# The bias tables of an attention mixer move out of the first feed-forward to the memory's keys, and 1/rms begins behind the second chunk

## The chip, the cores and the metric

The kernel runs on one core of one Trainium2 chip. The metric is the device time of one execution in microseconds (us), as the median of several runs of the same program.

## The reference

Two transformer layers over 512 positions of width 1024, with float32 tensors. What matters here:

```python
# layer 1
x = x + 0.5 * swiglu_ffn(rmsnorm(x, g1), w_in1, w_out1)        # f1, width 2816
h = rmsnorm(x, g_mix)
o_nsa  = nsa_attention(..., rel_bias)   # scores + rel_bias[rel_bucket(distance)]
o_conv = short_gated_conv(...)
o_mem  = memory_attention(...)          # keys and values from 256 memory rows
x = x + (g_nsa * o_nsa + g_conv * o_conv + g_mem * o_mem) @ w_out
x = x + 0.5 * swiglu_ffn(rmsnorm(x, g2), w_in2, w_out2)        # f2
# layer 2: sliding window and linear attention, memory attention, then
x = x + swiglu(rmsnorm(x, g3), w_gate, w_up, w_down)           # f3
return rmsnorm(x, g_final)
```

`rel_bias` has 32 buckets for 16 heads. A distance decides the bucket, so the bias of a head is one line of numbers over the distances, and the attention needs that line in each of 128 partitions.

## The kernel before

**Matmuls.** Each product is made of three, of the high and the low half of both sides (`mm3`, L233). A weight of 512 KB is fetched by SyncE's queue (SP) into one of three raw buffers, `wr`; ScalarE (ACT) casts its high half, `wh` (L260); the low half `wl` is a subtraction (L242) on VectorE (DVE), or, in the two mixers, on GpSimd (POOL) for two weights of three and on DVE for the third. TensorE (PE) then runs the matmuls, all recorded in line 231; `chunk` (L313) is one output tile of 24 matmuls. A scheduler lays out the order on each engine when the program is built; `tick` (L541) lets the next step of a list, `self.todo`, be written at that point, and `issue_after` holds a step until after a given matmul.

**Feed-forwards.** f1, f2 and f3 have one form (`ffn`, L688): three plain chunks (`plain`, L656), then 19 chunks as `unit` with fewer multiplications, whose weights `f_s` are summed by a second DMA on POOL's queue, and after each of three groups of chunks eight output products, which end in the DVE instruction `x<-u,x` (L254). The norm's 1/rms is made while the first chunks run: `rc` (L443) sums squares by eight small matmuls `o<-ones,acc`, and makes the root by some twelve small DVE instructions (`rsv`, `rs4t`, `rs4y`) and the cast `rsh` on ACT; `rb` (L449) spreads the result by matmuls with `identr`.

**Tables.** `tables` (L511) makes 16 steps, one after each of f1's chunks or output products. Eight are `line` steps for a quarter of a table: each opens a pool `tab`, sets and loads `rel` (POOL's queue, L520), loads a piece of the one-hot matrix `oh` (SP, L522), makes one product into the PSUM buffer `o`, copies it to `row` on DVE, and writes that to DRAM (`drel` or `dcmp`, POOL's queue, L527). Eight are `rows` steps: POOL's queue writes two heads' lines for 128 partitions, 640 KB, from `drel` to `dline` in DRAM (L533).

**Memory attention in the first mixer.** `mix1` (L1420) calls `mem_kv` (L867): eight chunks of keys (weights `m_km`), each scaled to `kr` and squared to `ksq`; eight pieces of weights for the values (`m_vm`); then the keys' own root of mean squares (`mem_rms`, matmuls `t<-im,ksq`, twelve DVE instructions, two transposes, `hr`) and eight matmuls `t<-hr,bm` that scale the keys. `mem_heads` (L958) then does scores, softmax and sums of four heads, with gate products from weights `m_gm` beside them.

## Time and profile before

| | us |
|---|---|
| median of three runs (2512.44, 2512.69, 2516.0) | 2512.69 |
| the profiled execution | 2515.75 |
| its span in the trace | 2514.0 |
| PE busy | 2373.9 |
| DVE, ACT, POOL busy | 1698.5, 1159.3, 442.9 |

The span is what the trace shows from the first instruction to the last, and 1.75 us of the profiled execution lie around it. In a row, the engine, the line and the operation are followed by the output tile and its inputs; an entry in square brackets is idle time before the instruction, with what ended it. PEclk is the granted clock of TensorE, 1.00 at 2.4 GHz and 0.50 at 1.2 GHz.

### The profile page before, as it was taken

The page shows a single profiled execution, that of the slowest core. Times are in us where ns is not written, and L with a number is a line of the kernel's source. Part 1 is how long each engine was busy: PE and PEld are TensorE (multiplying, and loading weights), DVE is VectorE, ACT ScalarE, POOL GpSimd, SP SyncE. Part 2 cuts the span into 40 slices and gives each one's busy share as a digit, 9 for nine tenths or more (in the row PEclk, how much of TensorE's full clock was granted, in tenths as well). Part 3 has the DMA queues.
Part 4 walks back from the last instruction along what each step waited for, and adds up shares of the span by engine and source line. Part 5 has one row for each costly group of instructions (what it writes and reads, how often), then busy time and mean ns, then how long its engine had stood idle before and what let it go on. Part 6 is the DMA issues. An engine that isn't in the chain of part 4 may idle for free.

```text
span 2514.0 us, 35498 instructions
## 1 busy us (share of the span) xinstructions
PE 2373.9 (94%) x13626; PEld 2054.5 (82%) x13626; DVE 1698.5 (68%) x3149; ACT 1159.3 (46%) x2072; POOL 442.9 (18%) x279
## 2 busy tenths in 40 slices
PE   8974999899999999999999999998999998999997
PEld 6864998797778887887899998787788887789997
DVE  6733778766487757777676776467877367866675
ACT  5412445344355444444553453454665345643453
POOL 1101000242122223222000001212121431000000
PEclk8986999999999999999999999999999999999999
DMA  6525554343122222223445554222222332545551
GB/s 180 171 82 134 160 148 148 98 146 99 56 80 70 75 64 73 74 68 126 126 148 142 157 142 128 74 66 70 67 68 75 115 122 76 136 145 147 157 140 61
DMA packets 100165, 277.45 MB, mean 110 GB/s; under 512 B 18403, under 2 KB 26923, under 8 KB 99868
## 3 DMA queue, kind: packets, MB, share of 16 engines
q1 hardware_dynamic: 82924, 239.81, 29.3%
q0 software_dynamic: 17072, 35.38, 7.4%
q8 instruction: 107, 1.75, 0.3%
q14 instruction: 62, 0.51, 0.1%
HBM read 268.69 MB, written 11.64 MB: 112 GB/s over the span
## 4 chain that ended last, share of the span: by engine, by line
PE 64%; DVE 10%; ACT 3%; issue 2%; DMA 1%; POOL 0%; DVEq 0%; ACTq 0%; POOLq 0%
PE g L231 36%; PE s L231 12%; PE t L231 11%; PE o L231 3%; PE t L239 2%; DVE wl L242 2%; ACT wh L260 1%; DMA wr<-f_s 1%; DVE qk L242 0%; DVE sp L1269 0%; DMA wr<-f_o 0%; DVE cv L254 0%; DVE sm L242 0%; ACT qk L260 0%; DVE o L254 0%
## 5 line engine op out<-in xcount | busy, mean ns | idle before, releaser
L231 PE MATMUL g<-xs,wh 128*128 128x512 f32 (+1 forms) x3022 | 886.4, 375 | 6.9 <-ACT wh L260 4.0
L260 ACT CAST wh<-wr 128x1024 fp32r<-128x1024 f32 (+6 forms) x405 | 409.7, 1015 | 625.3 <-PE g L231 209.1
L231 PEld LDWEIGHTS g<-xs,wh 128*128 128x128 f32 x3022 | 546.7, 191 | 97.7 <-ACT wh L260 7.2
L231 PE MATMUL g<-xs,wl 128*128 128x512 f32 (+1 forms) x1511 | 564.2, 373 | 1.4 <-POOL wl L242 1.2
L242 POOL TENSOR_TENSOR wl<-wr,wh 128x1024 fp32r<-128x1024 f32 (+4 forms) x135 | 313.8, 2325 | 901.3 <-ACT wh L260 671.6
L242 DVE TENSOR_TENSOR wl<-wr,wh 128x1024 fp32r<-128x1024 f32 (+5 forms) x270 | 326.8, 1211 | 81.8 <-ACT wh L260 79.6
L231 PEld LDWEIGHTS g<-xs,wl 128*128 128x128 f32 x1511 | 288.8, 191 | 52.2 <-issue 2.9
L231 PE MATMUL s<-xs,wh 128*128 128x256 f32 (+1 forms) x890 | 225.5, 341 | 8.0 <-ACT xs L260 2.0
L231 PE MATMUL t<-xs,wh 128*128 128x512 f32 (+1 forms) x888 | 224.1, 341 | 0.5 <-ACT e L260 0.4
L561 POOL DMA_DIRECT2D wr<-f_s x57 | 49.4, 872 | 775.8 <-DVE wl L242 174.1
L231 PEld LDWEIGHTS s<-xs,wh 128*128 128x128 f32 x890 | 154.2, 191 | 31.2 <-ACT wh L260 4.2
L231 PEld LDWEIGHTS t<-xs,wh 128*128 128x128 f32 x888 | 153.5, 190 | 20.1 <-ACT e L260 1.2
L231 PE MATMUL t<-xs,wl 128*128 128x512 f32 (+1 forms) x444 | 151.6, 341 | 2.7 <-DVE wl L242 2.7
L231 PE MATMUL s<-xs,wl 128*128 128x256 f32 (+1 forms) x445 | 151.2, 340 | 0.0
L257 ACT ACTIVATE sp<-sp,nm 128x128 f32<-128x128 f32 x192 | 101.9, 532 | 54.3 <-DVE nm L1269 41.5
L242 DVE TENSOR_TENSOR ptl<-t,pth 128x512 fp32r<-128x512 f32 (+1 forms) x128 | 73.4, 603 | 55.5 <-ACT pth L260 55.2
L260 ACT CAST pth<-t 128x512 fp32r<-128x512 f32 (+1 forms) x128 | 62.1, 520 | 92.7 <-PE t L239 92.3
L231 PE MATMUL g<-th,wh 128*128 128x256 f32 x308 | 86.6, 281 | 9.3 <-ACT wh L260 8.8
L231 PEld LDWEIGHTS t<-xs,wl 128*128 128x128 f32 x444 | 84.4, 190 | 13.2 <-DVE wl L242 4.0
L231 PEld LDWEIGHTS s<-xs,wl 128*128 128x128 f32 x445 | 85.0, 191 | 8.8
L231 PE MATMUL g<-th,wl 128*128 128x256 f32 x308 | 86.9, 282 | 1.6 <-DVE wl L242 1.5
L231 PE MATMUL g<-tl,wh 128*128 128x256 f32 x308 | 86.0, 279 | 0.0
(524 smaller groups left out, 4820.3 us busy)
## 6 DMA issues: line engine op xcount, KB each, us to landing
wr<-f_ab SPq DMA_DIRECT2D x73, 512.0 KB, 3.7
wr<-f_s SPq DMA_DIRECT2D x57, 512.0 KB, 3.6
wr<-f_s POOLq DMA_DIRECT2D x57, 512.0 KB, 7.0
wr<-f_o SPq DMA_DIRECT2D x48, 448.0 KB, 3.4
wr<-m_f SPq DMA_DIRECT2D x40, 512.0 KB, 3.6
wr<-m_o SPq DMA_DIRECT2D x40, 512.0 KB, 3.6
w<-f_ab SPq DMA_DIRECT2D x57, 256.0 KB, 4.2
wr<-f_o SPq DMA_DIRECT2D x24, 512.0 KB, 5.1
```

The source lines that it names most:

```text
L231: self.pm = self.nc.tensor.matmul(o, l, r, start=first, stop=last, skip_group_check=more)
L239: self.nc.tensor.transpose(o, i, self.ident)
L242: (e or self.nc.vector).tensor_tensor(o, x, y, op=op)
L257: return self.nc.scalar.activation(o, x, f, **k)
L260: return self.nc.scalar.copy(o, x)
L561: nc.gpsimd.dma_start(rs, a[key + "_s"][c][:, D:], accum_op=ALU.add)
```

## The change

**Tables.** `run` no longer puts the steps into f1. `mix1` opens one pool `tab` on the right around `mem_kv`, and eleven steps are written from there, one after each chunk of keys, and what is left behind the values. `rel` is loaded once, the two one-hot matrices come whole by SP, four matmuls (two of 320 columns, two of 512) go to the PSUM buffer `t`, four DVE copies make the tables, POOL's queue writes `drel` and `dcmp` once each, and the eight broadcasts `dline` follow.

**1/rms.** In all three feed-forwards `rc` stands behind both products of the second chunk, where it stood behind the first product of the third.

```diff
--- before.py
+++ after.py
@@ -508,23 +508,24 @@
         self.bg5 = self.t(g, [P, 16], F32, "bg5", 1)
         self.ts(self.bg5, self.cols[:, o:o + 16], 0.5, ALU.mult)
 
-    def tables(self):
+    def tables(self, p):
 
         nc, a = self.nc, self.a
-
-        def line(key, c, n, dst):
+        box = {}
+
+        def line(key, width, n):
             def go():
-                with self.pool("tab", "right") as p:
-                    rel = self.t(p, [33, 16], F32, "rel", 1)
-                    nc.vector.memset(rel, 1.0)
-                    nc.gpsimd.dma_start(rel[0:32], a["rel"])
-                    oh = self.t(p, [33, n], F32, "oh", 1)
-                    nc.sync.dma_start(oh, a["c_" + key][:, c:c + n])
-                    row = self.t(p, [16, n], F32, "row", 1)
-                    ps = self.ps("o", (16, n))
-                    self.mm(ps, rel, oh, True, True)
-                    nc.vector.tensor_copy(row, ps)
-                    nc.gpsimd.dma_start(dst[:, c:c + n], row)
+                if "rel" not in box:
+                    box["rel"] = self.t(p, [33, 16], F32, "rel", 1)
+                    nc.vector.memset(box["rel"], 1.0)
+                    nc.gpsimd.dma_start(box["rel"][0:32], a["rel"])
+                oh = self.load(key, pool=p)
+                box[key] = self.t(p, [16, 2 * width], F32, key + "l", 1)
+                for j in range(2):
+                    ps = self.ps("t", (16, width))
+                    s = slice(width * j, width * (j + 1))
+                    self.mm(ps, box["rel"], oh[:, s], True, True)
+                    nc.vector.tensor_copy(box[key][:, s], ps)
             return go
 
         def rows(j):
@@ -533,8 +534,11 @@
                 nc.gpsimd.dma_start(self.dline[s], self.drel[s, None, :].to_broadcast([2, P, LINE]))
             return go
 
-        st = [line("oh1", c, LINE // 4, self.drel) for c in range(0, LINE, LINE // 4)]
-        st += [line("oh2", c, 256, self.dcmp) for c in range(0, 1024, 256)]
+        def cmpline():
+            nc.gpsimd.dma_start(self.drel, box["oh1"])
+            nc.gpsimd.dma_start(self.dcmp, box["oh2"])
+
+        st = [line("oh1", LINE // 2, 2), line("oh2", 512, 2), cmpline]
         st += [rows(j) for j in range(8)]
         return st
 
@@ -653,7 +657,7 @@
         ul.append(l)
         self.tick()
 
-    def plain(self, p, key, c, uh, ul, rms):
+    def plain(self, p, key, c, uh, ul, lag):
 
         pa, pb = self.psf(), self.psf()
         if c == 0:
@@ -665,10 +669,10 @@
                     self.mm3(ps, h[:, s], l[:, s], self.xh[k], self.xl[k], k == 0, k == KT - 1)
         else:
             self.chunk(pa, key + "_ab", 2 * c, self.xh, self.xl)
-            if rms:
-                self.behind(lambda: self.rc)
             self.chunk(pb, key + "_ab", 2 * c + 1, self.xh, self.xl)
-        if rms:
+        if c == lag - 1:
+            self.behind(lambda: self.rc)
+        if c == lag:
             self.behind(lambda: self.rb)
 
         def act():
@@ -717,7 +721,7 @@
 
             wait, lag = [], 2
             for c in range(np_):
-                wait.append(self.plain(p, key, c, *parts[0], c == lag))
+                wait.append(self.plain(p, key, c, *parts[0], lag))
                 if c >= lag:
                     while wait:
                         wait.pop(0)()
@@ -874,6 +878,7 @@
                 self.chunk(ps, "m1_km", c, mh, ml)
                 k = self.t(q, [P, NMEM], F32, "kr", KT)
                 self.mul(k, ps, mrb)
+                self.tick()
                 kr.append(k)
                 s2 = self.t(q, [P, NMEM], F32, "ksq", 5)
                 self.act(s2, k, AF.Square)
@@ -1439,7 +1444,10 @@
                     qr = self.compressed()
                     self.tick(len(self.todo))
                 with self.pool("memkv") as kv:
-                    mem = self.mem_kv(kv)
+                    with self.pool("tab", "right") as tab:
+                        self.todo = self.tables(tab)
+                        mem = self.mem_kv(kv)
+                        self.tick(len(self.todo))
                     es.close()
                     self.mem_heads(*qr, *mem)
             self.rc5 = self.t(g, [P, 4], F32, "rc5", 1)
@@ -1932,7 +1940,6 @@
                 self.norm_sq(j)
             self.end_norm()
 
-            self.todo = self.tables()
             self.ffn("f1", 0.5, self.deferred(step, "mix", True), 3)
             self.upool.__exit__(None, None, None)
             done("d_f1")
```

What this moves on three engines, at the places where it matters. First POOL in the keys of the first mixer. Before, its queue there is a row of subtractions:

```order
L242 TENSOR_TENSOR wl_4952<-wr_4950,wh_4951 128x1024
L242 TENSOR_TENSOR wl_5023<-wr_5021,wh_5022 128x1024
L242 TENSOR_TENSOR wl_5058<-wr_5056,wh_5057 128x1024
L242 TENSOR_TENSOR wl_5129<-wr_5127,wh_5128 128x1024
L242 TENSOR_TENSOR wl_5170<-wr_5168,wh_5169 128x1024
```

In the change, from the second of its subtractions for the keys on:

```order
L242 TENSOR_TENSOR wl_4856<-wr_4854,wh_4855 128x1024
L538 DMA drel<-oh1l_4799 16x640
L242 TENSOR_TENSOR wl_4930<-wr_4928,wh_4929 128x1024
L534 DMA dline<-drel 256x1x640
L539 DMA dcmp<-oh2l_4843 16x1024
L534 DMA dline<-drel 256x1x640
L242 TENSOR_TENSOR wl_4966<-wr_4964,wh_4965 128x1024
L534 DMA dline<-drel 256x1x640 x2
L242 TENSOR_TENSOR wl_5039<-wr_5037,wh_5038 128x1024
L534 DMA dline<-drel 256x1x640
```

The writes of the tables and the broadcasts now stand between the subtractions, in the same queue; four broadcasts stand ahead of the subtraction `wl_5039` of the last key chunk, and four behind it, among those of the values.

Second, PE behind the memory's keys and values. Before, the sums for the keys' root (`im,ksq`) come behind the values, and gate products (`g` from `xs`) stand between them, the transposes (`ident,mr2y`) and the scaling products (`hr,bm`):

```order
L231 MATMUL t_5332<-im_120,ksq_5124 128x4
L231 MATMUL g_5422<-xs_3655,wh_5424 128x512
...
L231 MATMUL g_5422<-xs_3927,wh_5424 128x512
L239 MATMUL t_5356<-ident_112,mr2y_5343 4x128 x2
...
L231 MATMUL g_5456<-xs_3731,wh_5458 128x512
L231 MATMUL t_5361<-hr_5330,bm_3959 128x256
L231 MATMUL t_5368<-hr_5330,bm_3959 128x256
L231 MATMUL g_5456<-xs_3732,wh_5458 128x512
```

In the change they stand between the last key chunk and the values, with nothing between them:

```order
L231 MATMUL t_5243<-im_120,ksq_5034 128x4
L239 MATMUL t_5267<-ident_112,mr2y_5254 4x128 x2
L231 MATMUL t_5272<-hr_5241,bm_3839 128x256
L231 MATMUL t_5279<-hr_5241,bm_3839 128x256
...
L231 MATMUL t_5314<-hr_5241,bm_3839 128x256
L231 MATMUL t_5321<-hr_5241,bm_3839 128x256
L231 MATMUL g_5077<-wl_5081,mh_4098 128x512
```

The root's chain has moved ahead of the values, and its eight scaling products follow one another.

Third, DVE in f1, where `wl` and `l` are low halves of weights, `tl` of a form's weight, `ws` sums of a form, and `rsv` the first instruction of the root. Before:

```order
L242 TENSOR_TENSOR wl_543<-wr_531,wh_542 128x1024
L242 TENSOR_TENSOR tl_501<-ws_495,th_500 128x1024
L242 TENSOR_TENSOR ws_508<-sq_504 128x256
L242 TENSOR_TENSOR ws_508<-sq_506,sq_504 128x256
L254 SCALAR_TENSOR_TENSOR ws_508<-sq_506,ws_508 128x256
L242 TENSOR_TENSOR wl_639<-wr_630,wh_638 128x1024
L254 SCALAR_TENSOR_TENSOR ws_508<-ws_508,sq_506 128x256
L242 TENSOR_TENSOR l_653<-w_632,h_652 128x512
L251 TENSOR_SCALAR rsv_349<-o_344 128x8
L249 TENSOR_SCALAR rs4t_352<-rsv_349 128x8
```

In the change:

```order
L242 TENSOR_TENSOR wl_501<-wr_489,wh_500 128x1024
L251 TENSOR_SCALAR rsv_317<-o_312 128x8
L242 TENSOR_TENSOR tl_459<-ws_453,th_458 128x1024
L249 TENSOR_SCALAR rs4t_320<-rsv_317 128x8
L242 TENSOR_TENSOR wl_597<-wr_588,wh_596 128x1024
L251 TENSOR_SCALAR rs4y_319<-rs4t_320 128x8
L242 TENSOR_TENSOR ws_466<-sq_462 128x256
```

`rsv` has moved up to stand right behind the first `wl` of the unit, ahead of `tl` and of the second `wl`.

## Rows read from the trace of the kernel before

**Rows 1.** The page, parts 1 and 5: engines' busy us; the group of the casts, busy, mean ns.

```profile
PE 2373.9 (94%) x13626; PEld 2054.5 (82%) x13626; DVE 1698.5 (68%) x3149; ACT 1159.3 (46%) x2072; POOL 442.9 (18%) x279
...
L260 ACT CAST wh<-wr 128x1024 fp32r<-128x1024 f32 (+6 forms) x405 | 409.7, 1015 | 625.3 <-PE g L231 209.1
```

**Rows 2.** Waits of PE, 0 to 445 us: us in total, times, longest.

```profile
PE o L231 <- DMA rel<-rel: 38.0, 3, 17.5
```

**Rows 3.** Timeline of PE, 173 to 224.5 us: start, us, instruction, [idle before <- releaser].

```profile
196.11 1.01 PE L231 MATMUL o<-oh,rel 33*16 33x256 f32 x2 [17.53 <-DMA rel<-rel]
...
223.60 0.58 PE L231 MATMUL g<-th,wh 128*128 128x256 f32 x1 [8.80 <-ACT wh L260]
```

**Rows 4.** Busy time in windows, core 0: us, PE, PEld, DVE, ACT, POOL (x), PEclk, DMA share, GB/s.

```profile
180.00:200.00 20.00, 1.01 (x2) 0.13 (x2) 0.44 (x2) 0.00 (x0) 4.58 (x6) 0.50 0.30 100
223.60:230.20 6.60, 6.44 (x28) 6.09 (x29) 6.15 (x7) 3.16 (x4) 0.00 (x0) 0.50 0.54 173
```

**Rows 5.** Timeline of POOL, 174 to 224 us.

```profile
181.14 0.50 POOL L520 DMA_DIRECT2D rel<-rel  x1
181.63 1.08 POOL L533 DMA_DIRECT2D dline<-drel  x1
197.88 0.50 POOL L527 DMA_DIRECT2D dcmp<-row  x1 [15.16 <-DVE rel L519]
```

**Rows 6.** DMA issues, 174 to 222 us: engine, op, count, KB each, median us to landing.

```profile
dline<-drel POOLq DMA_DIRECT2D x5, 640.0 KB, 15.6
rel<-rel POOLq DMA_DIRECT2D x3, 2.0 KB, 14.1
```

**Rows 7.** Timelines of PE and DVE: last cast and first out-product of group 1, three feed-forwards.

```profile
51.04 0.41 PE L231 MATMUL o<-identr,rsl 128*128 128x128 f32 x1
...
300.22 0.68 DVE L254 SCALAR_TENSOR_TENSOR x<-u,x 128x512 f32<-128x512 f32 x1
...
1246.47 0.27 PE L231 MATMUL o<-identr,rsh 128*128 128x128 f32 x1
...
1424.96 0.69 DVE L254 SCALAR_TENSOR_TENSOR x<-u,x 128x512 f32<-128x512 f32 x1
...
2178.83 0.28 PE L231 MATMUL o<-identr,rsl 128*128 128x128 f32 x1
...
2364.03 0.69 DVE L254 SCALAR_TENSOR_TENSOR x<-u,x 128x512 f32<-128x512 f32 x1
```

**Rows 8.** Timelines of PE, then DVE, 37 to 49 us.

```profile
37.00 0.95 PE L231 MATMUL o<-ones,acc 128*128 128x2 f32 x8
...
48.60 0.48 PE L231 MATMUL o<-identr,rsh 128*128 128x128 f32 x1 [5.05 <-ACT rsh L260]
...
38.20 1.22 DVE L242 TENSOR_TENSOR wl<-wr,wh 128x1024 fp32r<-128x1024 f32 x1 [6.97 <-ACT wh L260]
...
43.68 0.16 DVE L251 TENSOR_SCALAR rsv<-o 128x8 f32<-128x8 f32 x1
```

**Rows 9.** Windows in the stage of the keys, then of the values.

```profile
536.00:560.00 24.00, 24.00 (x193) 23.58 (x192) 16.35 (x23) 13.36 (x21) 13.29 (x6) 1.00 0.50 156
560.00:580.00 20.00, 20.00 (x94) 16.65 (x92) 9.77 (x9) 9.49 (x11) 13.15 (x6) 1.00 0.65 204
```

**Rows 10.** DMA issues, 87 to 130 us, then 560 to 580 us.

```profile
wr<-f_o SPq DMA_DIRECT2D x7, 512.0 KB, 7.3
...
wr<-m_vm SPq DMA_DIRECT2D x3, 512.0 KB, 3.7
```

**Rows 11.** Timelines of ACT, then PE: last square of the keys, their root, first scores.

```profile
558.71 0.42 ACT L257 ACTIVATE ksq<-kr 128x256 f32<-128x256 f32 x1
...
579.30 1.84 PE L231 MATMUL t<-im,ksq 128*128 128x4 f32 x16
...
588.50 0.50 PE L231 MATMUL t<-hr,bm 64*128 64x256 f32 x2
...
602.16 0.39 PE L231 MATMUL s<-kmh,ql 128*128 128x256 f32 x1 [1.83 <-DVE ql L242]
```

## The prediction

> **What bounds the kernel now.** The page's first part comes first: PE is busy 94% of the span [rows 1], so time is won only where PE stands still or runs at the low clock, and lost where the change makes it do so. The waits of PE up to the end of f1 show where that is: 38.0 us in three waits, put down to `rel` [rows 2]. Its timeline tells the place: three pairs of small table products of 1.01 us, each behind one of these waits (17.53 us for the second), and then the next real matmul at 223.60, after 8.80 us more for a cast [rows 3]. That is a hole of 38.0 + 8.8 + 3 x 1.01 = 49.8 us. The windows show what the hole costs besides: the granted clock is 0.50 in it and still 0.50 in the 6.6 us behind it [rows 4], which at full clock would have taken half, so 3.3 us more.
>
> Why it waits is read on POOL's queue. The reload of `rel` is issued at 181.14 us in 0.50, right ahead of a broadcast that takes 1.08 [rows 5]. But it lands 14.1 us later in the median, beside five broadcasts in this stretch, which land after 15.6 us [rows 6]. So a transfer of 2 KB stands in line behind 640 KB ones, the next `line` step waits for it, there is one PSUM buffer `o`, and PE, which works in order, waits with it. The `f_s` sums of the following chunks are queued on POOL behind all that, so the cast comes late too.
>
> **The change, part by part.**
>
> *G1, the tables leave f1.* The hole is the lower bound: 49.8 + 3.3 = 53 us. The upper bound comes from the sister stages. From the last matmul of the norm's spread to the first output product of group 1 it takes 249.2 us in f1 (51.04 to 300.22), 178.5 in f2 and 185.2 in f3 [rows 7]; they do the same work without tables. So f1 loses 70.7 us against f2 and 64.0 against f3. Not all of that is the tables', since f1 also starts at the kernel's start. I take the smaller, **64 us**, with 53 and 71 as ends. It contains the table products themselves.
>
> *G2, 1/rms in f1.* The eight sums run at 37.00, but PE waits 5.05 us, to 48.60, for their cast [rows 8]. The DVE instruction `rsv` would have had its input at 38, and starts at 43.68, because two `wl`, a `tl` and sums of forms stand ahead of it. In the changed order it is right behind the `wl` that starts at 38.20 and ends at 39.42. That is up to 4.3 us earlier, but the twelve instructions behind it are still mixed with a `tl`, a `wl` and sums, so I take **2.5 us** of it, with ends 0 and 5.05. In f2 and f3 the sums only come one product earlier and PE has no such wait there: 0.
>
> *C1, the table products in the mixer.* A pair for 256 columns took 1.01 us at half the clock [rows 3], so 0.5 at full clock. There are 2 x 320 + 2 x 512 = 1664 columns, so **3.3 us** of PE, which has no idle time there to put them in (24.00 of 24.00 and 20.00 of 20.00 us busy, [rows 9]). They wait for `rel` and the one-hot matrices, which are issued well ahead of the keys.
>
> *C2, the keys' root in PE's order.* This is the largest price. Before, the sums end at 581.14 us and the first scaling product starts at 588.50 [rows 11], 7.4 us of DVE, transposes and ACT, all covered by gate products. In the changed order nothing stands there: PE waits those 7.4 us. Ahead of it the last chunk's scaling, square and sum were covered by the values and no longer are: three operations like the square's 0.42 us [rows 11] with their handovers, by estimate 2 us. Behind it eight products each wait for DVE to empty a `t` buffer; the square's 0.42 us for as many columns is the nearest row, so eight take at least 3.4, and I put 3.6 us on them. Together **13 us**; it could be 7 if the values' weights would have been late anyway, or 16.
>
> *C3, the clock behind such a hole.* After the hole of 49.8 us the low clock lasted 6.6 us [rows 4], which cost half its length, 3.3 us. With one hole at the root and some low clock at the heads I take **4.5 us**, with ends 0 and 8.
>
> *C4, the heads.* The changed order puts the scores of all four heads ahead of the gate products whose `wl` come late on POOL. A score already waited 1.83 us with gate products in between [rows 11]. Without them each head's softmax is open to PE: **5 us**, 0 to 12.
>
> *C5, the weights.* Two resources are asked for more. POOL's subtractions take 13.29 of 24 and 13.15 of 20 us [rows 9]; eight broadcasts at 1.08 us [rows 5] and two table writes at 0.50 fit into the rest. DMA was busy 0.50 and 0.65 by weights alone [rows 9] and 0.30 by broadcasts alone [rows 4], so the sum stays just below one. But beside broadcasts, weights landed after 7.3 us and not 3.7 [rows 10]. With three raw buffers, a landing of 7.3, a cast of 1.0 [rows 1] and a subtraction of 2.2 (13.29 us for six, [rows 9]) make 10.5 us for three weights, or 3.5 for one, where PE needs one each 2.9 (24 matmuls of the 193 that fill 24.00 us, about 3.0; the values are a little quicker): 0.6 us for some twelve weights, 7 us if all of it shows. Part of it passes under the hole of C2; I take **3 us**, 0 to 7.
>
> The Trainium skill (page DMA: Bandwidth & Descriptors, section Anatomy of one DMA, the SWDGE path) fits a transfer from GpSimd's queue as 2.0 us plus its bytes over 436 GB/s, which I estimate as 3.5 us for a broadcast; the rows say 15.6 with five in flight, about 9 us for each, so the row decides. By that fit C5 would vanish and the sum be 3 us lower. By the same page's rule that an engine takes turns between queues (section Queues, rings and completion order) all of the 7 us would show, and the sum be 4 us higher.
>
> The other moved issues hide: two loads on SP have no wait and are ahead of the keys; the eight one-hot loads, eight `rel` loads and eight writes leave the queues of f1.
>
> **The sum.** Gain 64 + 2.5 = 66.5; cost 3.3 + 13 + 4.5 + 5 + 3 = 28.8; net -37.7 us. The profiled execution's 2515.75 us would become 2478.0. It stands 3.06 us above the median, so against the median of 2512.69 the forecast is **2475 us**.
>
> **The rivals.**
>
> *R1, the mixer takes it for nearly nothing.* If PE finds other work ready, or the values' matmuls were going to wait for weights anyway, of the cost only C1, the 7.4 us of the root and little else stays, some 11 us: 66.5 - 11 = 55 less, 2457 us. For it: DVE and ACT are at most 68% and 56% busy in the keys' and values' stage [rows 9]. Against it: the order itself, in which nothing stands in the hole.
>
> *R2, f1 gives only the hole.* If f1's other excess belongs to its start, with weights and clock still to come, the gain is 53 and G2 gives 0: 53 - 28.8 = 24 less, 2489 us. For it: after the spread f1 works at a low clock, the spread's matmuls take 0.41 us where f2's take 0.27 [rows 7]. Against it: part of that low clock comes from the wait of G2.
>
> *R3, slower: POOL's queue holds the weights back.* In f1 nothing but small loads stood behind a broadcast; now `wl` of the weights do. If a broadcast kept POOL until it has drained, about 9 us each or 72 us for eight, plus C1 to C4 of 25.8, the cost is 98 against 66.5: 31 us more, **2544 us**. It decides from (66.5 - 25.8) / 8 = 5.1 us a broadcast. Against it: POOL issued the broadcast at 181.63 in 1.08 us, 0.49 us behind `rel`, though others were in flight, and its 15.16 us of idle time behind it are put down to a step of a table, not to the broadcast [rows 5].
>
> *R4, the change does nothing to f1.* If the cast that waits 8.8 us was late because of `f_s` alone, the hole would stay. The three waits named `rel` say otherwise [rows 2], and f2 and f3 have the same `f_s` and come to the same place 64 us sooner or more [rows 7]. It would give 2512.69 + 28.8, some 2541 us.
>
> **How the numbers follow.** My forecast with its terms' spread has a chance of 0.52, R1 0.20, R2 0.22, R3 0.05, R4 0.01. The range goes from 2450, just below R1, to 2495, just above R2, and leaves out R3, R4 and the far ends of terms. A measurement of this kernel can tell about 0.2% or 5 us from no change. Faster by more than that are the first three cases: 0.94. R4 and a heavy mix of R2 with C2 to C5 at their upper ends give 0.02 for no change. Slower is R3 with half a chance that it is past its point: 0.04.
>
> **What would show it.** Right: no `rel` wait in f1 and the way to group 1's first product near 185 us; PE idle for some 12 us between the last key chunk and the values, ended by DVE, and half clock behind it; `m_vm` landing in 5 to 7 us; scores waiting on ACT or DVE. Wrong: POOL's `wl` starting only when a broadcast has landed, a wait of PE on POOL of many us at every third weight, or a hole in f1 that stays. If f1 shows a distance well above 190 us, G1 is wrong; if the stage of keys and values grows by less than 12 us or by more than 40, the costs are.

## The result and the profile after

| | median us | lowest to highest, runs | ratio to before, 95% interval |
|---|---|---|---|
| before | 2512.44 | 2501.74 to 2516.0, 7 | |
| after | 2487.0 | 2481.44 to 2494.09, 7 | 0.9903 [0.9882, 0.9924] |

The change saves 25.4 us; the forecast was 37.7, and 2487.0 lies inside the range of 2450 to 2495. The profiled execution of after took 2481.44 us, the lowest of its runs, and that of before 2515.75, near the highest of its own. So the two traces lie 34.3 us apart where the medians lie 25.4 apart; I therefore compare stages, and the total only by the medians.

Page of after, part 1, beside [rows 1]:

```profile
PE 2370.2 (96%) x13618; PEld 2052.8 (83%) x13618; DVE 1693.0 (68%) x3138; ACT 1158.6 (47%) x2072; POOL 435.6 (18%) x266
```

PE's busy time is almost what it was; the share grew because idle time went. Where it went is read from the casts of the square roots (`rsh`), one at each norm. Trace of after, instructions of the tile `rsh`: duration, first and last start in us, shape. They are the mixing norm behind f1, the memory's norm, and f2:

```profile
L260 ACT CAST rsh<-rs4y x1: 194/194/194, 381.8 to 381.8; 128x4 fp32r<-128x4 f32 x1
L260 ACT CAST rsh<-rs2y x1: 192/192/192, 433.9 to 433.9; 128x2 fp32r<-128x2 f32 x1
...
L260 ACT CAST rsh<-rs4y x1: 191/191/191, 1211.3 to 1211.3; 128x4 fp32r<-128x4 f32 x1
```

The trace of before has them at 449.0, 501.2 and 1243.9. So f1 gains 67.3 us, and the way from the memory's norm to f2 grows from 742.7 to 777.4, by 34.7. From the last matmul of the norm's spread to the first output product of group 1 [rows 7] it now takes 184.9 us (48.0 to 232.9) for 249.2. f1's hole is closed. Waits of PE in after, 0 to 445 us, beside [rows 2]:

```profile
PE s L231 <- ACT wh L260: 4.1, 3, 3.1
...
PE o L231 <- ACT rsh L260: 2.2, 1, 2.2
```

No `rel` is left among them, and the wait on the root, 5.05 us before [rows 8], is 2.2.

The cost in the mixer lies whole in one stage: from the copy of the memory's 1/rms (`rmb`) to the last product of the heads with the values. It took 140.6 us before and takes 178.3, 37.7 more. The windows of this stage, of before and then of after (columns as in [rows 4]: window, length, busy time of PE, PEld, DVE, ACT, POOL, granted clock, DMA share, GB/s):

```profile
527.30:667.90 140.60, 136.64 (x754) 114.55 (x752) 82.09 (x167) 61.57 (x111) 43.29 (x18) 0.98 0.33 102
```

```profile
460.10:638.40 178.30, 149.14 (x750) 122.48 (x749) 79.85 (x171) 61.24 (x111) 52.17 (x28) 0.89 0.34 106
...
500.00:510.00 10.00, 4.37 (x22) 4.37 (x22) 0.00 (x0) 1.24 (x2) 6.79 (x4) 0.66 0.50 133
510.00:520.00 10.00, 2.50 (x12) 2.21 (x10) 3.55 (x7) 1.36 (x2) 3.35 (x2) 0.64 0.46 150
520.00:530.00 10.00, 6.02 (x14) 3.62 (x15) 7.38 (x24) 3.51 (x9) 0.00 (x0) 0.50 0.19 70
```

PE stands idle for 178.3 - 149.1 = 29.2 us, where it was 4.0, and is busy 12.5 us longer. Of that 3.6 are the table products; the other 8.9, by difference, are in the main the same work at a lower granted clock (0.89 in the mean against 0.98). The worst is 500 to 530, where PE works 12.9 of 30 us at 0.50 to 0.66. What ends the idle time, waits of PE in after, 440 to 620 us:

```profile
PE g L231 <- POOL wl L242: 6.7, 1, 6.7
PE t L231 <- DVE ksq L242: 6.6, 1, 6.6
PE s L231 <- ACT pm L257: 4.9, 7, 1.3
PE g L231 <- ACT wh L260: 3.4, 3, 2.3
PE t L239 <- DVE mr2y L254: 2.5, 1, 2.5
```

Before has three waits of PE in this stage: `ql` 1.8 us, `pm` 1.7 and `pm` 0.2.

The first is a weight that POOL subtracts late, the next is the end of the keys' squares, with `mr2y` the root behind them, `pm` are the heads. Why POOL is late stands on its own timeline (start, duration, instruction, idle time before it and what ended it):

```profile
484.92 1.09 POOL L534 DMA_DIRECT2D dline<-drel  x1 [0.27 <-issue]
...
488.39 1.09 POOL L534 DMA_DIRECT2D dline<-drel  x1
502.15 1.05 POOL L534 DMA_DIRECT2D dline<-drel  x1 [12.67 <-issue]
503.22 2.35 POOL L242 TENSOR_TENSOR wl<-wr,wh 128x1024 fp32r<-128x1024 f32 x1
```

Three broadcasts, the first at 482.92, go in 1.1 us each. The fourth is issued 12.67 us late, and what ended this idle time is "issue": POOL waited for nothing that the profile shows. The `wl` behind it starts at 503.22, and PE's product with it at 505.63, after the 6.67 us of the list. It goes on from there: the raw buffer of that weight comes free late, the next load (`m_vm`) is late, and ACT waits for it in order, with a key's square behind the cast:

```profile
512.96 1.04 ACT L260 CAST wh<-wr 128x1024 fp32r<-128x1024 f32 x1 [11.72 <-DMA wr<-m_vm]
513.91 0.41 ACT L257 ACTIVATE ksq<-kr 128x256 f32<-128x256 f32 x1
```

The key of this square was ready on DVE at 510.7, and PE's sum of the squares starts at 516.75, 6.56 us late. The theory after the result was therefore: f1 is as forecast, and what was too small is the weights' term, through broadcasts that hold POOL. Rivals were the root's place in PE's order, and the low clock by itself.

### The profile page after: what moved, and what is told of

Same layout as the page of the kernel before. It is cut to its first block, busy times and chain, and to the rows that moved or that the text cites. A ratio compares the mean times of both kernels' runs of the same rounds, so it can differ in the third digit from the quotient of the medians.

```text
span 2479.6 us, 35436 instructions
## 1 busy us (share of the span) xinstructions
PE 2370.2 (96%) x13618; PEld 2052.8 (83%) x13618; DVE 1693.0 (68%) x3138; ACT 1158.6 (47%) x2072; POOL 435.6 (18%) x266
## 4 chain that ended last, share of the span: by engine, by line
PE 65%; DVE 10%; ACT 3%; issue 2%; DMA 1%; POOL 1%; DVEq 0%; ACTq 0%; POOLq 0%
PE g L231 36%; PE s L231 12%; PE t L231 11%; PE o L231 3%; PE t L239 2%; DVE wl L242 2%; ACT wh L260 1%; DVE qk L242 1%; DMA wr<-f_s 0%; POOL wl L242 0%; DVE sp L1274 0%; DVE cv L254 0%; DMA wr<-m_gm 0%; DVE sm L242 0%; ACT qk L260 0%
```

## The experiments

### Each part of the change alone: e_tab and e_rc

`e_tab` has the change without the move of 1/rms, `e_rc` only that move:

```diff
-        if rms:
+        if c == lag - 1:
+            self.behind(lambda: self.rc)
+        if c == lag:
```

> Only the tables' move; 1/rms stands where it stood before. If the prediction's terms hold, 1/rms is worth 2.5 us and all of it in f1, so some 2489 us, 23 us less than before. If the 5 us that f3 was shorter in the profile of the change come from 1/rms, some 2495 us.

> Only 1/rms moved; the tables stay in f1. By the prediction's term PE waits some 2.5 us less for the cast of the root in f1, and nothing changes in f2 and f3: 2510 us, within 0.2% of before. If 1/rms is worth more in f3, 2505 us.

`e_tab`: 2483.44 us, ratio 0.9883 [0.9861, 0.9905], below both of its forecasts. `e_rc`: 2512.15, ratio 0.9993 [0.998, 1.0007]. In `e_tab` the casts of the roots stand at 48.8, 381.7, 433.9 and 1212.3: f1's first root is late as before, yet the mixing norm comes at the same 381.7 as in after. So the tables make the whole gain, and the 2.8 us that PE waits less on f1's root reach nothing: the later chunks take them up. In f3 the moved root comes 5.5 us earlier (75.7 us behind the last one, where before has 81.2), and the way from it to the next norm is 5.7 longer (322.3 against 316.6). So G2 is worth nothing that these runs can tell; the interval of `e_rc` leaves it at most 5 us.

### Was it the reload of `rel`? e_rel

Before, with `rel` loaded once and not ahead of each step:

```diff
+        rel = self.t(self.g, [33, 16], F32, "rel", 1)
+        nc.vector.memset(rel, 1.0)
+        nc.gpsimd.dma_start(rel[0:32], a["rel"])
```

> The kernel before, with rel loaded once at the start and kept, and nothing else changed: the tables stay in f1 by quarters, and so do the eight broadcasts on POOL's queue. Theory A (the hole in f1 is made by the reloads of rel that stand in line behind broadcasts): the three waits of 38.0 us go, PE does its table products without waiting, and the hole of 49.8 us shrinks to a few us, so some 45 us less than before, about 2465 us. Rival B (the broadcasts themselves hold what comes behind them on POOL's queue, the f_s sums above all): a hole of the same kind stays, now as waits for casts of f_s weights, and the gain is under 20 us, 2492 us or more.

2507.11 us, ratio 0.9983 [0.9972, 0.9993]: 4 or 5 us, not 38. The waits of PE, 0 to 445 us, and POOL's timeline in this kernel:

```profile
PE g L231 <- ACT wh L260: 37.7, 2, 37.2
```

```profile
178.18 2.18 POOL L533 DMA_DIRECT2D dline<-drel  x2 [0.25 <-issue]
191.24 1.06 POOL L533 DMA_DIRECT2D dline<-drel  x1 [10.88 <-issue]
...
195.17 1.89 POOL L561 DMA_DIRECT2D wr<-f_s  x2
```

The `rel` wait is gone and a wait on a cast of 37.2 us has its place. It is the same hole, ended by another: the `f_s` sums stand on POOL behind the broadcasts, which go out only after 10.88 us of "issue", and the two sums behind them land 18.5 us after they are issued, where after's at 192 and 197 us land in 7.7. So already before the change it was the broadcasts that held f1, and `rel`'s name in [rows 2] told only which of their victims came last. This also gives POOL's hold a second place.

### The broadcasts later, or on another queue: e_late and e_hw

`e_late` is after with the broadcasts tied behind a subtraction of POOL each, two in the heads and six in the attention stage; `e_hw` is after with the broadcasts on ACT's queue:

```diff
+                if h < 2:
+                    self.hold(self.rows.pop(0))
...
+                        self.todo, self.rows = st[:3], st[3:]
```

```diff
-                nc.gpsimd.dma_start(self.dline[s], self.drel[s, None, :].to_broadcast([2, P, LINE]))
+                nc.scalar.dma_start(self.dline[s], self.drel[s, None, :].to_broadcast([2, P, LINE]))
```

> The changed kernel, with the three table steps as they are, but the eight broadcasts held until later: two behind POOL's subtractions for the heads' gate weights, six one by one in the attention that follows. Theory A (in the mixer the fourth broadcast held POOL for 12.7 us, the key's low half behind it came late, and what followed stood in queues behind that): no idle POOL ahead of a subtraction, no wait of PE of 6.7 us for wl, none of 6.6 us for ksq; the way from the memory's root in front of the mixer to f2's root shrinks by some 25 of the 34.7 us that the change added there, about 2460 us. Rival B (the tables' loads, products and copies among the keys cost most of it): under 8 us, 2479 us or more.

> The changed kernel, with the eight broadcasts issued from ScalarE's queue and not from POOL's. Theory C (POOL is held by its own queue once three broadcasts are under way, 12.7 us in the change, and the low halves wl stand behind that): POOL's idle time ahead of the keys' wl goes, the waits of 6.7 us for wl and 6.6 us for ksq go, and the low clock of the table products stays, so some 20 us less than the change: about 2465 us. Rival D (the broadcasts' traffic stretches the weights' landing, from whatever queue): weights of the values still land after 6 us, PE still waits for casts, and the time stays within 8 us of the change, 2479 us or more.

`e_late`: 2546.65 us, ratio 1.0138 [1.0115, 1.0162], slower than before. In the keys' stage it does what it should: no `wl` waits behind a broadcast, and the root is covered by the values again. The stage takes 160.5 us, 17.8 less than in after. But from the first to the last `sp` of the attention behind it takes 525.6 us, where before and after have 446.3 and 444.5, with waits on other steps of that stage (15.3 us for `ptl`, 10.2 for `nm`): the moved issues brought the scheduler to another order there. The total therefore says nothing on the broadcasts, and the stage only a part: PE's order differs there too, so the 17.8 us belong to the broadcasts and to the covered root together. Theory A's 2460 us is missed, and the time lies on rival B's side for a reason that neither named.

It also shows the clock by itself. Windows of `e_late`:

```profile
474.00:480.00 6.00, 6.00 (x25) 4.88 (x26) 3.83 (x7) 3.21 (x5) 2.36 (x1) 0.50 0.00 1
...
485.00:490.00 5.00, 5.00 (x13) 1.88 (x11) 1.82 (x3) 1.67 (x3) 2.24 (x1) 0.50 0.05 14
```

PE is busy for every us and granted 0.50. The fall comes at some 467 us, behind 26 small sums of four columns (465.17, 3.66 us) and ten us ahead of the first table product (478.62). The same sums stand at the head of this stage in before and after, where the low clock behind them lasts some 4 and 7 us. From 464.9 to 495 the granted clock is 0.55 in the mean (by length: 9.1 us at 0.64, 16 at 0.50, 5 at 0.53), so some 13 us of the 30 are lost against full clock. There is no hole here that could be blamed; why it lasts so much longer here no run shows.

`e_hw`: 2512.88 us, ratio 0.9998 [0.9978, 1.0018], the whole gain lost: theory C had some 2465, rival D a time within 8 us of after. POOL is free, but now ACT is held. ACT's timeline with its queue (`ACTq`):

```profile
495.38 10.60 ACTq L534 DMA_DIRECT2D dline<-drel  x1
...
506.18 13.61 ACTq L534 DMA_DIRECT2D dline<-drel  x1
...
519.88 0.42 ACT L257 ACTIVATE ksq<-kr 128x256 f32<-128x256 f32 x1 [12.46 <-issue]
```

Two broadcasts go in 1.17 and 0.58 us; the third takes ACT 10.60 us and each one behind it 13 to 16, in plain sight, and a square waits 12.46. Theory C, that the hold is POOL's own, falls: it is the issuer's, whichever that is, once two or three of these are under way.

### The clock: e_clk

`e_late` with the table products' left side filled up to 128 columns (112 of them unused):

```diff
-                    box["rel"] = self.t(p, [33, 16], F32, "rel", 1)
+                    box["rel"] = self.t(p, [33, P], F32, "rel", 1)
```

> The kernel with the late broadcasts, and its four table products made with a left side of 128 columns (16 of the tables, 112 unused), so that they fill the array's columns. The stretch from the memory's root to the end of the keys is what counts. Theory E (products with 16 columns leave TensorE so little used that the clock of 0.50 is kept up from the small sums before them until 5 us behind the last of them, 26 us in all): the granted clock returns to 1.00 ahead of the table products or soon behind them, and the last key is scaled some 8 to 13 us sooner than 44.8 us behind the root. Rival F (the clock falls for another reason, the products' type or their 33 rows): no change, 44 us or more.

One run, 2546.86 us, as `e_late`. The last key is scaled 42.0 us behind the root's copy, where `e_late` has 44.8: between the two forecasts. The low clock ends some 5 us earlier, but so do the table products: it outlasts the last of them (to 490.3 in `e_late`, 484.8 here) by some 4.5 us in both. The windows of `e_clk`:

```profile
485.00:490.00 5.00, 5.00 (x27) 5.00 (x27) 0.60 (x2) 0.20 (x1) 0.51 (x1) 0.57 0.32 118
490.00:495.00 5.00, 5.00 (x44) 5.00 (x43) 1.97 (x4) 2.53 (x4) 2.41 (x1) 1.00 0.07 29
```

But here the clock had come back to 1.00 for some us ahead of the products, which it had not in `e_late`, and PE waited 1.50 us for DVE among them. So the run doesn't tell whether the fuller products or that pause made the difference. What keeps the clock down stays open.

### The mixer left alone: e_best and e_half

`e_best` is after with the table products at the program's start, their one-hot matrices loaded through ACT's queue, and the eight broadcasts issued behind the last `f_s` sum of f1; nothing of the tables is left in the mixer. `e_half` is the same with sixteen broadcasts of one head (320 KB) for eight of two (640 KB):

```diff
+        with self.pool("tab", "right") as tab:
+            st = self.tables(tab)
+            for f in st[:3]:
+                f()
+        self.rows = st[3:]
...
+                    if last and self.rows:
+                        self.hold(self.rows.pop(0))
...
-                        self.todo = self.tables(tab)
```

```diff
-                s = slice(2 * j, 2 * j + 2)
+                s = slice(j, j + 1)
```

> The changed kernel, with the table products at the program's very start, where PE waits for its first weights (one-hot matrices by ScalarE's queue), and all eight broadcasts behind the last f_s sum of f1, where POOL has nothing to do until the mixer. If tables cost where they share a busy stretch of PE or stand ahead of work on POOL, then the mixer is as it was before (716.5 us from the memory's root to f2's root) and f1 is as short as in the change: some 30 us less than the change, about 2452 us. POOL issues three broadcasts at once and then one per some 9 us (theory C), or all eight in 1.1 us each (against it). If the start is delayed by the products: 2456 us.

> As the one before, with sixteen broadcasts of one head (320 KB) in place of eight of two. If POOL is held by the number of transfers under way, it stops after the third or fourth, at half the bytes; if by their descriptors or bytes, it stops after six or seven. The whole time as the one before, within 5 us.

`e_best`: 2460.83 us, ratio 0.9789 [0.9762, 0.9816], 50.8 us below the runs of before beside it (2511.61) and the best kernel of this study. From the memory's norm to f2 it takes 734.4 us, so the mixer has its old time back (742.7 in before, 739.0 in `e_rc`). It loses at the start: the first real matmul begins at 26.02, after 13.84 us of waiting on ACT, where `e_tab` has 7.41, and the mixing norm comes at 402.0, not 381.8. A better start could give back at most these 20 us; no run tried it alone.

`e_half`: 2465.01 in one run, within `e_best`'s 2456.33 to 2464.65 but for 0.4 us. Its trace shows something else. POOL's timeline and the transfers from 306 to 360 us, of `e_best` (two heads) and then of `e_half` (one head):

```profile
306.31 3.58 POOL L546 DMA_DIRECT2D dline<-drel  x3
328.34 1.06 POOL L546 DMA_DIRECT2D dline<-drel  x1 [18.46 <-issue]
...
DMA packets 10369, 12.37 MB, mean 229 GB/s; under 512 B 7423, under 2 KB 7423, under 8 KB 10235
```

```profile
306.33 4.00 POOL L546 DMA_DIRECT2D dline<-drel  x7
...
DMA packets 3655, 13.12 MB, mean 243 GB/s; under 512 B 528, under 2 KB 528, under 8 KB 3521
```

The same bytes go in a third of the packets. What is missing are packets that carry next to nothing: of 512 B and more there are 2946 with two heads and 3127 with one. POOL is not held for 18 us, and all sixteen are issued by 323 us instead of 352. That gave the next theory: not the broadcast, but its form is what the weights paid for.

### The form of the broadcast alone: e_a1, e_b1, e_r1

`e_a1` is after with each broadcast issued as two of one head, and nothing else. `e_b1` is before with the same edit, `e_r1` is `e_b1` with `rel` loaded once:

```diff
-                s = slice(2 * j, 2 * j + 2)
-                nc.gpsimd.dma_start(self.dline[s], self.drel[s, None, :].to_broadcast([2, P, LINE]))
+                for h in range(2 * j, 2 * j + 2):
+                    s = slice(h, h + 1)
+                    nc.gpsimd.dma_start(self.dline[s], self.drel[s, None, :].to_broadcast([1, P, LINE]))
```

> The changed kernel with each broadcast of two heads (640 KB) issued as two of one head (320 KB), and nothing else. The run before this one showed sixteen of one head drained in some 20 us where eight of two take over 45. Theory G (the form of the broadcast, small packets at 100 GB/s, is what holds POOL and whatever stands behind it in the keys): POOL's idle time of 12.7 us ahead of the fourth broadcast goes, with PE's waits of 6.7 us for wl and 6.6 us for ksq; the root's chain and the table products with their low clock stay. Some 15 to 20 us less than the change, about 2468 us. Rival H (the order of PE and the clock cost it, and the broadcasts are only in the neighbourhood): within 5 us of the change, 2482 us or more.

> The kernel before, with each broadcast of two heads issued as two of one head, and nothing else: tables by quarters in f1, rel reloaded each time on POOL's queue. Theory G: rel and f_s have little to stand behind, rel lands after some 3 to 6 us, and the three waits of 38.0 us shrink to under 12; with the late cast behind them the hole of 49.8 us shrinks by 30 us or more: 2480 us or less. Rival I (the hole is made by the chain of loads, products and writes by quarters itself): under 10 us, 2502 us or more.

> As the one before, and rel loaded once. If theory G holds, this leaves of the tables in f1 only the products, the waits for pieces of oh and the low clock around them: 5 to 15 us less than the one before, about 2470 us, and the mixer is untouched. If the pieces of oh take over as the wait, it equals the one before.

`e_a1`: 2471.91 us, ratio 0.9845 [0.9823, 0.9867], 40.6 below the runs of before beside it (2512.54) and 15 below after. POOL's timeline where after has its hold:

```profile
487.09 1.58 POOL L535 DMA_DIRECT2D dline<-drel  x3
488.69 2.41 POOL L242 TENSOR_TENSOR wl<-wr,wh 128x1024 fp32r<-128x1024 f32 x1
491.04 2.07 POOL L535 DMA_DIRECT2D dline<-drel  x4
```

Transfers from 482 to 560 us of `e_a1`, and of after in the fence behind it. The second line of each is POOL's queue (packets, MB, the time of its packets as a share of the time of 16 DMA engines), the third the broadcasts (issued by, KB each, median us to landing):

```profile
DMA packets 3364, 12.73 MB, mean 163 GB/s; under 512 B 517, under 2 KB 517, under 8 KB 3361
...
q0 software_dynamic: 1335, 5.34, 21.3%
...
dline<-drel POOLq DMA_DIRECT2D x16, 320.0 KB, 6.2
```

```profile
DMA packets 10136, 12.28 MB, mean 157 GB/s; under 512 B 7398, under 2 KB 7398, under 8 KB 10134
...
q0 software_dynamic: 8150, 5.02, 20.9%
...
dline<-drel POOLq DMA_DIRECT2D x8, 640.0 KB, 18.7
```

The small packets are not what takes the time. From 2 to 8 KB there are 2736 packets in after and 2844 in `e_a1`, so these carry the data in both, and POOL's queue takes the same share of the DMA engines' time, 20.9% and 21.3%, for like bytes. What differs is how much of the engines it keeps busy while the broadcasts are under way: 32.5% from 484 to 504 us in after (1.94 MB), 62.1% from 486 to 500 in `e_a1` (2.69 MB). So two heads in one transfer are spread over fewer engines at a time and land later. That this is what holds POOL is argued, not shown: packets and spread change together.

The hold is gone, and with it PE's wait on POOL's `wl`; the wait on `ksq` falls from 6.6 to 4.5, in two parts, so most of it is the root's. And the stage, with the columns of above:

```profile
462.60:627.60 165.00, 145.37 (x750) 119.88 (x749) 79.86 (x171) 61.31 (x111) 52.32 (x36) 0.92 0.35 114
```

165.0 us against 178.3, so the two-head form costs 13.3 us there: 9.5 of idle time and 3.8 of low clock. PE's order in this stage is that of after. 24.4 us above before remain. Between 510 and 520 PE is busy 5.17 of 10 us at 0.50: the root still stands open.

`e_b1`: 2492.57, ratio 0.9917 [0.9892, 0.9942], between its two forecasts; `e_r1`: 2492.48, ratio 0.9925 [0.9906, 0.9944]. With the tables where they were, the form alone saves 20 us in all, and 16.1 of f1's 67 by the mixing norm (432.9 us for 449.0). The waits of PE to 445 us, of `e_b1` and then `e_r1`:

```profile
PE g L231 <- ACT wh L260: 19.3, 3, 18.0
PE o L231 <- DMA rel<-rel: 14.6, 3, 5.6
```

```profile
PE g L231 <- ACT wh L260: 21.9, 1, 21.9
```

`rel` falls from 38.0 to 14.6, and without its reloads the same time is again waited for the cast, since a row of broadcasts still stands ahead of the `f_s` sums on POOL. So the place had to change as well as the form; the edits don't stand for each other.

### A combination that failed: e_final

From `e_half`, with the products moved from the program's start into f1, their one-hot matrices loaded by SP, and each of the sixteen broadcasts behind one `f_s` sum:

```diff
-        with self.pool("tab", "right") as tab:
...
+        if self.rows:
+            self.hold(self.rows.pop(0))
...
+            with self.pool("tab", "right") as tab:
+                st = self.tables(tab)
...
+            self.rows = st[3:]
             self.ffn("f1", 0.5, self.deferred(step, "mix", True), 3)
```

> All that the runs point to in one kernel: 1/rms as in the change; the table products inside f1's first chunk, behind the first weights, from one pool that closes before the forms; sixteen broadcasts of one head, each behind one f_s sum of f1 on POOL's queue; the mixer without any of it. If the price of the tables is their products with the low clock (some 8 us where PE runs full, less at the start) and little else, f1 loses under 10 us against the change's f1, the mixer is as before (about 735 to 743 us from the memory's root to f2's), and the whole takes about 2450 us. If the broadcasts between the f_s sums stretch these, f1 loses 20 us or more and the whole takes 2465 us or more, as long as the version with all of it at the start.

2537.53 us, ratio 1.0104 [1.0086, 1.0122], slower than before. The mixer is left alone (740.6 us from the memory's norm to f2), but f1 is drawn out: its mixing norm comes at 477.4, not 381.8. POOL's timeline of `e_final`, and behind it that of `e_tab`:

```profile
93.35 0.86 POOL L572 DMA_DIRECT2D wr<-f_s  x1 [15.21 <-DMA wr<-f_s]
93.92 0.85 POOL L541 DMA_DIRECT2D dline<-drel  x1
109.51 0.85 POOL L572 DMA_DIRECT2D wr<-f_s  x1 [14.75 <-DVE t L242]
```

```profile
67.34 0.86 POOL L565 DMA_DIRECT2D wr<-f_s  x1 [11.12 <-DVE e L242]
77.53 0.86 POOL L565 DMA_DIRECT2D wr<-f_s  x1 [9.33 <-DVE u L254]
```

The sums come every 16 us and not every 10, though each broadcast takes POOL 0.85 us and lands after 5.7 in the median. PE waits little at a time, but at every chunk (12.7 us on casts in 14 waits, 12.5 in 13). What ties each sum to the broadcast ahead of it was not settled: a semaphore that they share, or the order of the chunk's raw loads. It stays open.

## Why the prediction was right and wrong, point by point

**G1, right, and shown.** 64 us forecast between 53 and 71; 67.3 by the mixing and memory norms, in after and in `e_tab` alike. The sign named for it came: 184.9 us to group 1's first product, forecast near 185. The sister stages were the right ruler: they gave 64 to 70.7, while the hole alone [rows 3, 4] would have said 53. R2, which held f1's excess for its own start, falls. The reason given was half of it: `rel` alone was not what had to go (`e_rel`), but the broadcasts, which held everything that stood behind them on POOL.

**G2, the mechanism right, the gain not there.** The wait fell from 5.05 to 2.2 us as forecast (2.5), but its end moves nothing (`e_rc`, and `e_tab` beside after). A wait that ends on the path counts only if what stands behind it does not wait again; that step was missing.

**The costs, 28.8 forecast, 37.7 measured in the keys' and values' stage.** Term by term, from the rows of after less those of before:

| term | forecast (ends) | after | from |
|---|---|---|---|
| C1 products | 3.3 | 3.6 | rows of 0.71, 1.02 and 1.89 us for the eight |
| C2 root | 13 (7 to 16) | 11.6 | waits: `ksq` 6.6, `mr2y` 2.5, `kr` 1.6, `hr` 0.9 |
| C3 clock | 4.5 (0 to 8) | 8.9 | busy 149.1 - 136.6, less C1 |
| C4 heads | 5 (0 to 12) | 3.2 | `pm` 4.9, before 1.7 |
| C5 weights | 3 (0 to 7) | 10.1 | `wl` of POOL 6.7 and `wh` 3.4, before neither |
| other waits | none | 0.3 | rest of 25.2 us of idle time |

The rows of a wait name the last releaser, so the table understates what the broadcasts did: 2.1 us of `ksq` and 3.8 of the clock go with them too. `e_a1` takes the hold away and measures it whole: with it gone the stage costs 24.4 us, 3.2 of them waits for `wh`, and C1 to C4 were forecast at 25.8. So C5 is the step that failed: the two-head broadcasts alone cost 13.3 us, where the whole term was put at 3 with an upper end of 7.

The sentence in it that failed is "eight broadcasts at 1.08 us ... fit into the rest", and with it the argument against R3, that POOL let one go in 1.08 us with others in flight [rows 5]. That row is true and says nothing on the next ones: in after, too, three go in 1.1 us each, and the fourth waits 12.67. The "[15.16]" of idle time behind the broadcast, which I put down to a table step, should have been followed to its neighbours in the same stage; `e_rel`, which takes the table step's `rel` away, has 10.88 us of "issue" there. R3's mechanism was real, and its sign came: `wl` stood until a broadcast had landed or nearly so, for the fourth goes out 19.2 us behind the first, and a broadcast lands after 18.7. But the eight cost 13.3 us together, 1.7 each, where it would decide from 5.1. What R3 says of f1, that nothing but small loads stood behind a broadcast there, was wrong: the `f_s` sums did (`e_rel`).

I also took a broadcast's 15.6 us of landing as given by its bytes. The Trainium skill (page DMA: Bandwidth & Descriptors, section Anatomy of one DMA, the SWDGE path) would make it 3.5 us by an estimate; the measurement decides, 18.7 us in the median here, and the fit doesn't hold for the two-head form. The same page's table of specifications says that transfers under 512 B don't reach the line rate. The rows of this case don't bear that out as the cause: two heads bring many packets under 512 B, but the data goes in about as many larger ones with either form, and in the same time of the DMA engines. Yet one head lands after 6.2 us, with twice as many transfers of half the size. The sign stood in [rows 4]: with hardly anything but broadcasts to move, the DMA engines were busy 0.30 at 100 GB/s. I used it only to say that the sum of the shares stays below one.

**C3, the mechanism right, the holes miscounted.** The term had one hole, at the root. After has two, and the low clock stands behind both; `e_a1` has the root's alone. Windows of after behind its two holes, and of `e_a1` behind its one:

```profile
505.00:515.00 10.00, 4.57 (x22) 4.37 (x22) 1.07 (x2) 1.36 (x2) 4.88 (x4) 0.67 0.60 172
515.00:535.00 20.00, 13.32 (x39) 9.74 (x40) 11.50 (x31) 4.60 (x10) 4.48 (x3) 0.54 0.31 102
```

```profile
508.60:522.60 14.00, 9.07 (x26) 6.21 (x26) 9.80 (x30) 3.59 (x10) 0.00 (x0) 0.51 0.08 23
```

PE's busy time by the share of the clock that was not granted gives the loss, by estimate: 4.57 x 0.33 + 13.32 x 0.46 = 7.6 us in after, 9.07 x 0.49 = 4.4 in `e_a1`, which is the term's 4.5. Holes don't explain all low clock: in `e_late` it is 0.50 with PE fully busy. The cause of that stays open.

**C2 and C4 right** in mechanism and size: PE waits at the root on DVE's squares and `mr2y`, and in the heads on `pm`. Of C2's 11.6 us 2.1 are the hold's, 9.5 are left in `e_a1`. R1, the mixer for nearly nothing, falls with them. `e_late` bears it out from the other side: with the values behind the keys again, the waits on `ksq` and `mr2y` are gone.

**The total.** By the stages f1's 67.3 less the stage's 37.7 make 29.6; the medians show 25.4, with an interval of 19 to 30. Of the 12 us between forecast and result 8.9 are the costs, and the rest is within what runs of one kernel differ by.

## What to carry to other kernels

A transfer that is issued in a microsecond can still stop its issuer a few issues later, and then everything in that engine's order waits: move such transfers to where nothing stands behind them, and look first whether they leave most of the DMA engines idle while they are under way, since their form can be cheaper to change than their place. A named wait (`rel`) is the last of several victims of the same queue; taking it away alone shows whether it was the cause. And where a stage has sisters that do the same work without the suspected part, their difference is a better ruler for the gain than the visible hole.

The best kernel here takes the tables out of the mixer (`e_best`, 0.9789); the smallest edit beside the change is the one-head broadcast (`e_a1`, 0.9845).

## What was unexpected of the hardware

- A broadcast from DRAM to DRAM of two heads in one DMA brings thousands of packets under 512 B (7423 of 10369 in `e_best`'s stretch), the same of one head doesn't (528 of 3655). They cost no more time of the DMA engines (20.9% with two heads, 21.3% with one, after and `e_a1`); but two heads keep 32.5% of the engines busy while under way, one head 62.1%. Why is open.
- POOL let three of 640 KB go before it was held, for 12.67 us in after and 18.46 in `e_best`; of 320 KB seven went in one stretch in `e_half`. The fourth of 640 KB went 19.2, 22.0 and 15.7 us behind the first (after, `e_best`, `e_rel`), where a broadcast lands after 18.7, 21.4 and 15.7 in the median: as if it waited for the first to land. ACT's queue was held from the third on, 10.6 to 16 us each.
- The granted clock was 0.50 for 16 us on end with PE busy throughout (`e_late`, 474 to 490).
